# A head's block inverse in one visit to TensorE: four steps for four successive heads at once, in turn by rows

## The chip, the cores and the metric

The kernel runs on one core of a Trainium2 chip, as one launch. The metric is the device time of that launch in microseconds (us). A core has five engines with a queue of instructions each: PE (TensorE, the matrix products; its weight loads are listed apart as PEld), DVE (VectorE), ACT (ScalarE), POOL (GpSimd) and SP (SyncE, which issues the DMAs here). An engine works through its queue in order and waits on semaphores for results of the others.

## What is computed

The program is a trunk of two layers over 512 positions of width 1024. In each layer a gated delta-rule branch (8 heads of width 128) and a sliding-window attention branch run side by side, are merged, and a feed-forward part follows. The change lies in the delta rule, whose core in the reference is a pair of triangular solves for each head and chunk of positions:

```python
kb = k * beta[..., None]
L = jnp.where(strict, jnp.einsum('bhnid,bhnjd->bhnij', kb, k) * decay, 0.0)
u = lax.linalg.triangular_solve(L, v * beta[..., None], left_side=True,
                                lower=True, unit_diagonal=True)
w = lax.linalg.triangular_solve(L, kb * jnp.exp(g)[..., None], left_side=True,
                                lower=True, unit_diagonal=True)
...
def step(state, inp):
    qd, kd, u_c, w_c, a_c, gl = inp
    v_new = u_c - jnp.einsum('bhcd,bhde->bhce', w_c, state)
    o = (jnp.einsum('bhcd,bhde->bhce', qd, state)
         + jnp.einsum('bhij,bhje->bhie', a_c, v_new))
    state = state * jnp.exp(gl)[..., None, None] + jnp.einsum('bhcd,bhce->bhde', kd, v_new)
    return state, o
```

## The kernel before

**The inverse.** The kernel cuts the 512 positions into four chunks (NC = 4) of 128 and builds, for each head and chunk, the inverse of a unit triangular 128x128 matrix, stored as the tile `Pt` (128 x 512, the four chunks side by side). The 32x32 inverses on the diagonal of all heads are made beforehand by `solve`, and stand in `Pc` and, transposed, in `Tc`. The matrix itself (`uu`) lies in DRAM (`ud`). From these parts `d_prep(h)` puts one head's inverse together in four steps. Each step is a group of small fp32 products on TensorE into a bank of PSUM, followed by VectorE instructions that bring the result to SBUF:

- z1 (L964): eight 32x32 products, off-diagonal block times `Tc`, for the rows 0 to 31 and 64 to 95; copied to `zz` (L967).
- p1 (L971, L975): twelve 32x32 products of `zz` with `Pc`; they give the off-diagonal parts of the 64x64 inverses, written to `Pt` (L980) and, transposed, to `T64` (L977).
- z2 (L985): four 64x64 products of the off-diagonal 64x64 block with `T64`, copied to `z2` (L988).
- p2 (L991): four 64x64 products of `z2` with `Pt`; the result is written to the last quarter of `Pt` (L993).

Each step needs the one before, so between two of them TensorE does other work. I call a run of such products between other TensorE work a visit: a head has four. Which rows of the array a product uses is set by the partitions where its operands lie (0, 32, 64 or 96), and the partitions of its output set the columns. `d_prep` also loads `ur` (the head's matrix), `D` and `kk`, clears `Pt` and `T64` on GpSimd and copies the diagonal blocks in, and ends with four transposes of the keys (`ps_kt`, L1000), which ScalarE scales into `kd`.

**The loop over heads.** For head h the code runs `d_prep(h + 1)`, then `d_chain(h)`, the recurrence over four chunks, then steps of the tails of earlier heads, then `d_dense(h + 1)`, three projections of 24 large products each (`ps_qp`, `ps_vp`, `ps_zp`). `d_chain` begins with `ps_qk` (L1067) and transposes of v (`ps_vt`, L1076), and goes on chunk by chunk: y (L1095, which needs `Pt`), su (L1100) and o (L1107), then ks (L1089) and another product into o (L1090). Between two links of this chain VectorE has to bring a result to SBUF.

**What sets the order.** A scheduler orders each engine's instructions when the kernel is built, by priorities and its own estimate of times; what is written one after the other is interleaved. So the large products of `d_dense(h + 1)` stand between the links of `d_chain(h)` and, before, between the visits of `d_prep(h + 1)`. The helper `Order` fixes the order of an engine's instructions between `begin` and `end`, relative to each other.

**Buffers.** PSUM has a bank `pk` (PK, one buffer), which the four steps and `ps_kt` take in turn; `ps` (PS, three), `ss` (PZ, two; `ps_o` is there) and `pm` (PM, two, for the projections). In SBUF `T[2]` has four buffers (`Pt` and `ur`), `X4` six of twice that size. Weights are loaded by SP (`wr`), split by ScalarE (`wh`) and VectorE (`wl`) and used four chunks later at most.

Of the kernel before, what the change touches and what calls it, by code (L numbers as in the profile page):

```python
# [10 lines left out]
F32 = mybir.dt.float32  # L11
# [4 lines left out]
ALU = mybir.AluOpType  # L16
# [103 lines left out]
def hybrid_trunk(ctx, tc, x, positions, pre_mix_g, dn_conv_w, dn_a_log, dn_dt_bias, dn_norm_g,  # L120
# [70 lines left out]
    def c4(ap):  # L191
        return ap.rearrange("p (c i) -> p c i", c=4)
# [67 lines left out]
    def umat(h):  # L260
        return ud[h * NC:(h + 1) * NC, 0:P * P].rearrange("c (j i) -> j c i", j=P)
# [231 lines left out]
    for l in range(depth):  # L493
# [440 lines left out]

        dn = {}

        def d_prep(h):

            Pt = T[2]("Pt")
            nc.gpsimd.memset(Pt, 0.0)  # L940
            T64 = sm.tile([64, 256], F32, name="T64", bufs=1)
            nc.gpsimd.memset(T64, 0.0)
            Ptv, T6v = c4(Pt), T64.rearrange("p (c n) -> p c n", c=4)
            ah = slice(h * NC, (h + 1) * NC)
            ur = T[2]("ur")
            dma(c4(ur), umat(h))
            urv = c4(ur)
            d, k_ = T[3]("D"), T[3]("kk")
            dma(d, dd[h])
            dma(k_, kkd[h])  # L950
            for b in range(4):
                r = slice(b * 32, (b + 1) * 32)
                nc.gpsimd.tensor_copy(Ptv[r, :, r], Pcv[r, ah, :])
            for b in range(2):
                r = slice(b * 32, (b + 1) * 32)
                nc.gpsimd.tensor_copy(T6v[r, :, r], Tcv[r, ah, :])
            yield
            zz = sm.tile([P, 4, 64], F32, name="zz", tag="zz", bufs=2)
            v4 = lambda a: a.rearrange("p (c n) -> p c n", c=4)
            halves = [(slice(b, b + 32), slice(b + 32, b + 64)) for b in (0, 64)]  # L960
            psq = PK("ps_z1")
            for r0, r1 in halves:
                for c in range(NC):
                    mm(psq[r1, c * 32:c * 32 + 32], lhsT=urv[r0, c, r1],  # L964
                       rhs=Tcv[r0, h * NC + c, :], start=True, stop=True)
            for r0, r1 in halves:
                nc.vector.tensor_copy(zz[r1, :, 0:32], v4(psq[r1, 0:128]))  # L967
            psq = PK("ps_p1")
            for r0, r1 in halves:
                for c in range(NC):  # L970
                    mm(psq[r0, c * 32:c * 32 + 32], lhsT=zz[r1, c, 0:32],  # L971
                       rhs=Pcv[r1, h * NC + c, :], start=True, stop=True)
            r1 = halves[0][1]
            for c in range(NC):
                mm(psq[r1, 128 + c * 32:160 + c * 32], lhsT=Pcv[r1, h * NC + c, :],  # L975
                   rhs=zz[r1, c, 0:32], start=True, stop=True)
            ts(out=T6v[r1, :, 0:32], in0=v4(psq[r1, 128:256]), scalar1=-1.0, scalar2=None,  # L977
               op0=ALU.mult)
            for r0, r1 in halves:
                ts(out=Ptv[r0, :, r1], in0=v4(psq[r0, 0:128]), scalar1=-1.0, scalar2=None,  # L980
                   op0=ALU.mult)
            lo_, hi_ = slice(0, 64), slice(64, 128)
            psq = PK("ps_z2")
            for c in range(NC):
                mm(psq[hi_, c * 64:c * 64 + 64], lhsT=urv[lo_, c, hi_], rhs=T6v[lo_, c, :],  # L985
                   start=True, stop=True)
            z2 = sm.tile([P, 4, 64], F32, name="z2", tag="zz", bufs=2)
            nc.vector.tensor_copy(z2[hi_], v4(psq[hi_, 0:256]))  # L988
            psq = PK("ps_p2")
            for c in range(NC):  # L990
                mm(psq[lo_, c * 64:c * 64 + 64], lhsT=z2[hi_, c, :], rhs=Ptv[hi_, c, hi_],  # L991
                   start=True, stop=True)
            ts(out=Ptv[lo_, :, hi_], in0=v4(psq[lo_, 0:256]), scalar1=-1.0, scalar2=None,  # L993
               op0=ALU.mult)
            kds = sm.tile([P, NC], F32, name="kds")
            tc.keep_in_program_order(tt(out=kds, in0=cj[h], in1=c4(d)[:, :, P - 1], op=ALU.mult))
            ps = PK("ps_kt")
            for c in range(NC):
                sl = slice(c * P, (c + 1) * P)
                tr(ps[:, sl], k_[:, sl], ident)  # L1000
# [4 lines left out]
            dn["p", h] = Pt, d, k_, kd  # L1005

        def d_dense(h, after=lambda: None):
            egb = T[6]("egb")
# [50 lines left out]
                    next(tails[h], None)  # L1059

        def d_chain(h):
            Pt, d, k_, kd = dn.pop(("p", h))
            qq, qe, wq, vv, sz = dn.pop(("d", h))
            ps = PS("ps_qk")
            for c in range(NC):
# [300 lines left out]
```

## Time and profile before

| | |
|---|---|
| median of 3 runs | 1878.03 us (1876.44 to 1878.68) |
| profiled execution, own time | 1874.57 us |
| its span, first to last instruction | 1872.9 us |
| mean granted TensorE clock | 0.999 |
| head loop, layer 0 and layer 1 | about 303 to 480 us, 1230 to 1410 us |
| instructions on DVE, ACT, POOL | 2466, 1913, 385 |

A line of the profile names the source line (L964), the engine, the operation, the tiles as output<-inputs (buffer numbers and often digits at the end of a name left out, so that `ps_z` stands for ps_z1 and ps_z2, `ps_p` for ps_p1 and ps_p2, `z` for z2, `T` for T64), the shape and a count. A tile name alone does not tell steps apart; the line does.

### The profile page before, as it was taken

What the parts mean: (1) busy time and instruction counts of PE and PEld (TensorE: products, weight loads), DVE (VectorE), ACT (ScalarE), POOL (GpSimd) and SP (SyncE); (2) the same over time, 40 slices, a digit from 0 to 9 for tenths busy, and PEclk for the clock granted to TensorE, in tenths of its full rate; (3) what the DMA queues carried; (4) which work ended last, traced back from release to release, by engine and by line L of the source; (5) the groups of instructions that cost most, each with busy time, mean ns of one, the idle gap of its engine ahead of it and who ended that gap; (6) DMA issues with size and microseconds to landing.
All of it is one profiled execution on the core that took longest, in us unless ns stands there. A gap on an engine that the chain in (4) does not pass through costs nothing. (4 is left out here: it accounts for less than half of the span.)

```text
span 1872.9 us, 26807 instructions
## 1 busy us (share of the span) xinstructions
PE 1847.6 (99%) x9716; PEld 1534.1 (82%) x9716; DVE 1281.5 (68%) x2466; ACT 939.7 (50%) x1913; POOL 208.1 (11%) x385
## 2 busy tenths in 40 slices
PE   8999999999999999999999999999999999999998
PEld 7888788888888888888888887888888888888886
DVE  5499795777656667684556997857775667586834
ACT  6678732344434645454356887233333346454442
POOL 1322102121100000000012221022111000000000
PEclk9999999999999999999999999999999999999999
DMA  5633436333363253544245333553433533534631
GB/s 179 202 115 117 120 125 196 102 119 109 86 215 127 91 188 97 176 168 170 83 143 188 103 126 105 160 173 102 125 97 110 194 124 99 183 114 158 205 119 45
DMA packets 123445, 255.40 MB, mean 136 GB/s; under 512 B 32609, under 2 KB 49313, under 8 KB 123314
## 3 DMA queue, kind: packets, MB, share of 16 engines
q1 hardware_dynamic: 123314, 253.71, 42.0%
q8 instruction: 76, 1.25, 0.3%
q14 instruction: 55, 0.45, 0.1%
HBM read 224.70 MB, written 28.97 MB: 135 GB/s over the span
## 5 line engine op out<-in xcount | busy, mean ns | idle before, releaser
L320 DVE TENSOR_TENSOR wl<-wr,wh 128x1024 fp32r<-128x1024 f32 (+1 forms) x332 | 402.6, 1222 | 331.2 <-ACT wh L319 323.4
L319 ACT CAST wh<-wr 128x1024 fp32r<-128x1024 f32 (+1 forms) x332 | 344.1, 1041 | 561.8 <-PE ps_f L336 145.9
L335 PE MATMUL ps_f<-g_h,wh 128*128 128x512 f32 x448 | 174.3, 389 | 0.0
L336 PE MATMUL ps_f<-g_l,wh 128*128 128x512 f32 x448 | 174.3, 389 | 0.0
L337 PE MATMUL ps_f<-g_h,wl 128*128 128x512 f32 x448 | 174.3, 389 | 0.0
L397 PE MATMUL ps_p<-wl,P_h 128*128 128x512 f32 x336 | 131.2, 391 | 0.8 <-DVE wl L320 0.8
L399 PE MATMUL ps_p<-wh,P_l 128*128 128x512 f32 x336 | 130.8, 389 | 0.0
L395 PE MATMUL ps_p<-wh,P_h 128*128 128x512 f32 x336 | 129.5, 389 | 0.0
L434 POOL TENSOR_TENSOR pr<-pq,pw 128x1 f32<-128x1 f32 x16 | 9.3, 583 | 809.5 <-DVE pq L433 809.5
L336 PEld LDWEIGHTS ps_f<-g_l,wh 128*128 128x128 f32 x448 | 84.1, 188 | 17.5
L335 PEld LDWEIGHTS ps_f<-g_h,wh 128*128 128x128 f32 x448 | 84.1, 188 | 17.4
L337 PEld LDWEIGHTS ps_f<-g_h,wl 128*128 128x128 f32 x448 | 84.1, 188 | 17.4
L397 PEld LDWEIGHTS ps_p<-wl,P_h 128*128 128x128 f32 x336 | 63.1, 188 | 15.6 <-DVE wl L320 2.3
L395 PEld LDWEIGHTS ps_p<-wh,P_h 128*128 128x128 f32 x336 | 63.1, 188 | 13.3 <-ACT wh L319 0.2
L399 PEld LDWEIGHTS ps_p<-wh,P_l 128*128 128x128 f32 x336 | 63.1, 188 | 12.8
L382 PE MATMUL ps_b<-wh,h_h 128*128 128x432 f32 (+1 forms) x192 | 71.1, 371 | 0.0
L383 PE MATMUL ps_b<-wl,h_h 128*128 128x432 f32 (+1 forms) x192 | 70.4, 367 | 0.0
L384 PE MATMUL ps_b<-wh,h_l 128*128 128x432 f32 (+1 forms) x192 | 70.0, 366 | 0.0
L285 DVE TENSOR_TENSOR wr<-wr 128x1024 f32<-128x1024 f32 x48 | 58.0, 1221 | 2.4 <-DMA wr<-in_weights_dram 1.9
L335 PE MATMUL ps_qp<-h_h,wh 128*128 128x512 f32 x128 | 54.9, 429 | 0.0
L336 PE MATMUL ps_qp<-h_l,wh 128*128 128x512 f32 x128 | 54.1, 423 | 0.0
L864 ACT ACTIVATE M<-M,nm 128x128 f32<-128x128 f32 x128 | 49.8, 391 | 5.9 <-DVE nm L859 5.9
(356 smaller groups left out, 4855.4 us busy)
## 6 DMA issues: line engine op xcount, KB each, us to landing
wr<-in_weights_dram SPq DMA_DIRECT2D x308, 512.0 KB
wr<-in_weights_dram SPq DMA_DIRECT2D x24, 432.0 KB
D<-dd SPq DMA_DIRECT2D x32, 256.0 KB
xd<-xo SPq DMA_DIRECT2D x12, 512.0 KB
xt<-xd SPq DMA_DIRECT2D x24, 256.0 KB
D<-gd SPq DMA_DIRECT2D x16, 256.0 KB
dd<-D SPq DMA_DIRECT2D x16, 256.0 KB
kkd<-kk SPq DMA_DIRECT2D x16, 256.0 KB
```

The costliest lines, as they stand in the source:

```text
L285: tt(out=a, in0=a, in1=o, op=ALU.add)
L319: nc.scalar.copy(wh[:, :w], wr[:, :w])
L320: sub(out=wl[:, :w], in0=wr[:, :w], in1=wh[:, :w].bitcast(F32), op=ALU.subtract)
L335: mm(ps, lhsT=wh[:, k, :], rhs=hi, start=k == 0, stop=False)
L336: mm(ps, lhsT=wh[:, k, :], rhs=lo, start=False, stop=False)
L337: mm(ps, lhsT=wl[:, k, :], rhs=hi, start=False, stop=k == KT - 1)
L382: mm(pss[t], lhsT=hi[:, tsl], rhs=wh[:, r, :], start=k == 0, stop=False)
L383: mm(pss[t], lhsT=hi[:, tsl], rhs=wl[:, r, :], start=False, stop=False)
L384: mm(pss[t], lhsT=lo[:, tsl], rhs=wh[:, r, :], start=False, stop=k == KT - 1)
L395: mm(pss[t], lhsT=hi[:, c], rhs=wh[:, r, :], start=first, stop=False, skip_group_check=onto)
L397: mm(pss[t], lhsT=hi[:, c], rhs=wl[:, r, :], start=False, stop=False, skip_group_check=onto)
L399: mm(pss[t], lhsT=lo[:, c], rhs=wh[:, r, :], start=False, stop=last, skip_group_check=onto)
```

## The change

`d_prep` is split into `d_load` (the loads of a head's matrix), `d_inverse` (the four steps) and `d_keys` (loads of `D` and `kk`, and `ps_kt`). One call `d_inverse(h)` makes, in one bank `ps_i` and one more (`pst`, for the product that is needed transposed), z1 of head h + 3, p1 of head h + 2, z2 of head h + 1 and p2 of head h. The products of z2 and p2 come first, one of each in turn; then those of z1 and p1, in turn by rows. `Order` keeps them in this order. A head's steps so lie in four successive calls, and the calls go from h = -3 to 7; those at the ends hold only the steps whose head exists. `T64` is one tile for the whole program, cleared once. The matrices of up to four heads are held in two `X4` tiles.

```diff
@@ constants
+    T64 = const.tile([64, 256], F32, name="T64")
+    nc.gpsimd.memset(T64, 0.0)
+    T6v = T64.rearrange("p (c n) -> p c n", c=4)
@@ in place of d_prep(h)
+        urs = [X4("ur") for i in range(2)]
+        uview = lambda h: c4(urs[h // 2 % 2][:, h % 2 * 512:(h % 2 + 1) * 512])
+        lo_, hi_ = slice(0, 64), slice(64, 128)
+        r0, r1, r2, r3 = (slice(b * 32, (b + 1) * 32) for b in range(4))
+        v4 = lambda a: a.rearrange("p (c n) -> p c n", c=4)
+        def d_load(*hs):
+            for h in hs:
+                if h < H:
+                    dma(uview(h), umat(h))
+        def d_inverse(h):
+            has = lambda g: 0 <= g < H
+            blk = lambda t_, g, r, c: t_[r, g * NC + c, :]
+            psq, pst = PK("ps_i"), PZ("ps_i")
+            u1, u2 = (uview(g) if has(g) else None for g in (h + 3, h + 1))
+            z1, z2, Pt = dn.get(("z1", h + 2)), dn.get(("z2", h)), dn.get(("p", h))
+            def wide(k):
+                return slice(256 + k * 32, 288 + k * 32)
+            order = Order(nc.tensor)
+            order.begin()
+            for c in range(NC):
+                cw_ = slice(c * 64, (c + 1) * 64)
+                if has(h + 1):
+                    mm(psq[hi_, cw_], lhsT=u2[lo_, c, hi_], rhs=T6v[:, c, :], start=True, stop=True)
+                if has(h):
+                    mm(psq[lo_, cw_], lhsT=z2[hi_, c, :], rhs=c4(Pt)[hi_, c, hi_], start=True, stop=True)
+            for c in range(NC):
+                if has(h + 3):
+                    mm(psq[r1, wide(c)], lhsT=u1[r0, c, r1], rhs=blk(Tcv, h + 3, r0, c), start=True,
+                       stop=True)
+                if has(h + 2):
+                    mm(psq[r0, wide(c)], lhsT=z1[r1, c, 0:32], rhs=blk(Pcv, h + 2, r1, c), start=True,
+                       stop=True)
+                if has(h + 3):
+                    mm(psq[r3, wide(c)], lhsT=u1[r2, c, r3], rhs=blk(Tcv, h + 3, r2, c), start=True,
+                       stop=True)
+                if has(h + 2):
+                    mm(pst[r1, c * 32:c * 32 + 32], lhsT=blk(Pcv, h + 2, r1, c), rhs=z1[r1, c, 0:32],
+                       start=True, stop=True)
+                    mm(psq[r2, wide(c)], lhsT=z1[r3, c, 0:32], rhs=blk(Pcv, h + 2, r3, c), start=True,
+                       stop=True)
+            order.end()
+            if has(h):
+                ts(out=c4(Pt)[lo_, :, hi_], in0=v4(psq[lo_, 0:256]), scalar1=-1.0, scalar2=None,
+                   op0=ALU.mult)
...
+            if has(h + 2):
+                ah = slice((h + 2) * NC, (h + 3) * NC)
+                Pt = T[2]("Pt")
+                dn["p", h + 2] = Pt
+                nc.gpsimd.memset(Pt, 0.0)
...
+        def d_keys(h):
...
@@ the loop
-        fin(d_prep(0))
+        d_load(0, 1, 2, 3)
+        for h in (-3, -2, -1):
+            d_inverse(h)
+        d_keys(0)
         for h in range(H):
+            d_inverse(h)
+            d_load(h + 4)
             if h < H - 1:
-                fin(d_prep(h + 1))
+                d_keys(h + 1)
             d_chain(h)
```

The lines after the change stand three further down in the shared code (L335 becomes L338); in `d_inverse`, L969 is z2, L971 p2, L974 and L980 z1, and L977, L983 and L985 p1; L1025 is `ps_kt`, L1093 `ps_qk`, L1102 `ps_vt`, L1121 y.

TensorE's order before, in layer 0, from the end of the projections for head 1: the inverse of head 2 is put together while head 1's chain starts.

```order
L337 MATMUL ps_zp<-h_h,wl 128x512
L964 MATMUL ps_z_3748<-Tc,ur 32x32 x8
L1067 MATMUL ps_qk<-qq,kk 128x128 x4
L971 MATMUL ps_p_3759<-Pc,zz 32x32 x8
L975 MATMUL ps_p_3759<-zz,Pc 32x32 x4
L1076 MATMUL ps_vt<-ident,vv 128x128 x4
L335 MATMUL ps_qp<-h_h,wh 128x512
L336 MATMUL ps_qp<-h_l,wh 128x512
L337 MATMUL ps_qp<-h_h,wl 128x512
L1095 MATMUL ps_y<-vs,Pt 128x128
L985 MATMUL ps_z_3775<-T_3733,ur 64x64 x4
```

The four runs of small products are apart; the fourth (L991) follows four large products later. After the change the visit h = 2 stands at the end of the projections for head 2. Its 64x64 products end and its 32x32 products begin like this (`z_3803` is z2 of head 2, `z_3805` z1 of head 4):

```order
L969 MATMUL ps_i<-T_96,ur 64x64
L971 MATMUL ps_i<-Pt,z_3803 64x64
L974 MATMUL ps_i<-Tc,ur 32x32
L977 MATMUL ps_i<-Pc,z_3805 32x32
L980 MATMUL ps_i<-Tc,ur 32x32
L983 MATMUL ps_i<-z_3805,Pc 32x32
L985 MATMUL ps_i<-Pc,z_3805 32x32
L974 MATMUL ps_i<-Tc,ur 32x32
```

Before the first row stand six more of the two lines in turn, and behind the last the rest of four rounds of five; nothing lies between. TensorE then goes on with head 2's chain and the transposes of head 3's keys:

```order
L985 MATMUL ps_i<-Pc,z_3805 32x32
L1093 MATMUL ps_qk<-qq,kk 128x128 x4
L1102 MATMUL ps_vt<-ident,vv 128x128 x4
L338 MATMUL ps_qp<-h_h,wh 128x512
L339 MATMUL ps_qp<-h_l,wh 128x512
L340 MATMUL ps_qp<-h_h,wl 128x512
L338 MATMUL ps_qp<-h_h,wh 128x512
L339 MATMUL ps_qp<-h_l,wh 128x512
L340 MATMUL ps_qp<-h_h,wl 128x512
L1025 MATMUL ps_kt<-ident,kk 128x128 x4
L1121 MATMUL ps_y<-vs,Pt 128x128
```

The small products have left the space between qk and y, and `ps_kt`, which takes the same bank as `ps_i`, follows six large products after vt. On VectorE the instructions that empty the bank now follow one another, here for the visit h = 2, between sz (from the projection `ps_zp`) and the first use of `ps_qk`:

```order
L410 TENSOR_TENSOR w_l<-w,w_h 128x512
L1047 SCALAR_TENSOR_TENSOR sz<-sz,ps_zp 128x512
L989 TENSOR_SCALAR Pt<-ps_i 64x4x64
L993 COPY z_4071<-ps_i 64x256
L998 COPY z_4073<-ps_i 32x128 x2
L1009 TENSOR_SCALAR T_96<-ps_i 32x4x32
L1012 TENSOR_SCALAR Pt<-ps_i 32x4x32 x2
L1021 TENSOR_TENSOR kds<-cj,D 128x4
L1097 SCALAR_TENSOR_TENSOR aT<-ps_qk,cj,D 128x128 x4
```

Before, instructions of these sizes stood in four places of VectorE's order, with those for `ps_qk` and y between them.

More of the change, by code (lines that the diff above doesn't have):

```diff
@@ new lines, in hybrid_trunk @@
+        lo_, hi_ = slice(0, 64), slice(64, 128)
[40 more added lines that the diff above has]
+                   op0=ALU.mult)
+            if has(h + 1):
+                z2 = sm.tile([P, 4, 64], F32, name="z2", bufs=1)
+                nc.vector.tensor_copy(z2[hi_], v4(psq[hi_, 0:256]))
+                dn["z2", h + 1] = z2
+            if has(h + 3):
+                z1 = sm.tile([P, 4, 32], F32, name="z1", bufs=1)
+                for r in (r1, r3):
+                    nc.vector.tensor_copy(z1[r], v4(psq[r, 256:384]))
+                dn["z1", h + 3] = z1
+            if has(h + 2):
[3 more added lines that the diff above has]
+                nc.gpsimd.memset(Pt, 0.0)
+                for r in (r0, r1, r2, r3):
+                    nc.gpsimd.tensor_copy(c4(Pt)[r, :, r], Pcv[r, ah, :])
+                for r in (r0, r1):
+                    nc.gpsimd.tensor_copy(T6v[r, :, r], Tcv[r, ah, :])
+                ts(out=T6v[r1, :, 0:32], in0=v4(pst[r1, 0:128]), scalar1=-1.0, scalar2=None,
+                   op0=ALU.mult)
+                for ra, rb in ((r0, r1), (r2, r3)):
+                    ts(out=c4(Pt)[ra, :, rb], in0=v4(psq[ra, 256:384]), scalar1=-1.0, scalar2=None,
+                       op0=ALU.mult)
@@ L950, in d_prep @@
             dma(k_, kkd[h])
[L951 to L992, printed above, removed]
@@ L1061, in d_chain @@
         def d_chain(h):
-            Pt, d, k_, kd = dn.pop(("p", h))
+            Pt = dn.pop(("p", h))
+            d, k_, kd = dn.pop(("k", h))
             qq, qe, wq, vv, sz = dn.pop(("d", h))
```

14 lines of the change are left out of this document (1 added, 13 removed).

## The prediction

> **What bounds the kernel now.** I read the page's line of engines first, then the view of windows over the two stages in which the edited code runs (the loop over the eight heads, once per layer).
>
> ```profile
> span 1872.9 us, 26807 instructions
> PE 1847.6 (99%) x9716; PEld 1534.1 (82%) x9716; DVE 1281.5 (68%) x2466; ACT 939.7 (50%) x1913; POOL 208.1 (11%) x385
> ```
>
> The windows give length, then busy time of PE, PEld, DVE, ACT and POOL, then granted clock and DMA.
>
> ```profile
> 303.00:480.00 177.00, 177.00 (x1287) 143.70 (x1285) 126.06 (x262) 67.91 (x136) 32.89 (x63) 1.00 0.35 109
> 1230.00:1410.00 180.00, 180.00 (x1299) 146.14 (x1299) 127.05 (x264) 69.33 (x138) 31.65 (x62) 1.00 0.36 110
> ```
>
> TensorE is busy for 177 of 177 us and 180 of 180 us, at full clock; VectorE, the next, for 126 of 177. So in these stages the start of each TensorE instruction sets the start of the next, and what counts is not how long a product lasts but how far apart the starts stand. That is read from the timeline of TensorE alone: start, length from first start to last end, line, shape, count. An fp32 product shows as two instructions (passes), so eight of them are x16. Head 0, with its four visits:
>
> ```profile
> 303.30 0.39 PE L337 MATMUL ps_ga<-h_h,wl 128*128 128x512 f32 x1
> 303.62 0.59 PE L964 MATMUL ps_z<-Tc,ur 32*32 32x32 f32 x16
> 304.14 1.16 PE L1067 MATMUL ps_qk<-qq,kk 128*128 128x128 f32 x8
> 305.23 0.49 PE L971 MATMUL ps_p<-Pc,zz 32*32 32x32 f32 x13
> 305.53 0.21 PE L975 MATMUL ps_p<-zz,Pc 32*32 32x32 f32 x1
> 305.56 0.19 PE L971 MATMUL ps_p<-Pc,zz 32*32 32x32 f32 x1
> 305.59 0.19 PE L975 MATMUL ps_p<-zz,Pc 32*32 32x32 f32 x1
> 305.59 0.19 PE L971 MATMUL ps_p<-Pc,zz 32*32 32x32 f32 x1
> ...
> 305.65 0.32 PE L975 MATMUL ps_p<-zz,Pc 32*32 32x32 f32 x5
> 305.90 0.66 PE L1076 MATMUL ps_vt<-ident,vv 128*128 128x128 f32 x4
> ...
> 307.09 0.39 PE L335 MATMUL ps_qp<-h_h,wh 128*128 128x512 f32 x1
> 307.32 0.40 PE L336 MATMUL ps_qp<-h_l,wh 128*128 128x512 f32 x1
> 307.65 0.68 PE L985 MATMUL ps_z<-T,ur 64*64 64x64 f32 x8
> 308.25 0.50 PE L337 MATMUL ps_qp<-h_h,wl 128*128 128x512 f32 x1
> 308.59 0.40 PE L335 MATMUL ps_qp<-h_h,wh 128*128 128x512 f32 x1
> ...
> 310.79 0.60 PE L1000 MATMUL ps_kt<-ident,kk 128*128 128x128 f32 x4
> ```
>
> Undisturbed, a large product starts 0.23 after the one before (307.09 to 307.32). Around a visit there are two losses: entering (307.32 to 307.65 is 0.33, so 0.10) and leaving (308.25 to 308.59 is 0.34, so 0.11), and inside the visit the last start stands well before the next user's.
>
> **What the four visits cost now.** For the lengths of single instructions, and to see that z2 and p2 are alike, the view by source line (ns min/median/max):
>
> ```profile
> L1067 PE MATMUL ps_qk<-qq,kk x128: 270/275/377, 304.1 to 1417.3; 128*128 128x128 f32 x128
> L964 PE MATMUL ps_z<-Tc,ur x256: 191/191/212, 303.6 to 1391.1; 32*32 32x32 f32 x128
> L985 PE MATMUL ps_z<-T,ur x128: 218/218/267, 307.6 to 1395.0; 64*64 64x64 f32 x128
> L991 PE MATMUL ps_p<-Pt,z x128: 218/218/267, 309.4 to 1396.7; 64*64 64x64 f32 x128
> ```
>
> And the pace of the 128x128 products, from a narrower window:
>
> ```profile
> 304.69 0.61 PE L1067 MATMUL ps_qk<-qq,kk 128*128 128x128 f32 x4
> ```
>
> Four qk passes last 0.61, one alone 0.275, so they stand 0.112 apart, and eight undisturbed would take 0.90 to the next start and be 1.06 long.
> - z1: enter 0.32 - 0.23 = 0.09; run 303.62 to 304.14 = 0.52; leave 0.10 (the qk row is 1.16 long, not 1.06). 0.71.
> - p1: enter 0.09 (qk holds 1.09, less 0.90, less the 0.10 just counted); run 305.23 to 305.90 = 0.67; leave 0.06 (vt row 0.66 against 0.60 of the kt row, four transposes each). 0.82.
> - z2: 0.10 + 0.60 + 0.11 = 0.81. p2: the same instruction lengths and form, 0.81.
>
> That is 3.15 us a head, 16 heads: **50.4 us**.
>
> **What the new visits cost.** Inside a run, starts follow the rows of the array. The z2 row is 0.68 long with a last pass of 0.22: eight passes on one row group start within 0.46, and 0.14 passes until the next user. At 305.65 five 32-row passes on one row group are 0.32 long, the last 0.19: 0.032 apart. But where two row groups alternate (305.59 twice, one L971 and one L975) two starts fall within 0.03: each group keeps its own pace, beside the other.
> - 64-row part of a full visit: the z2 and p2 products lie on the two halves of the rows, in turn. I take them side by side: 0.46 for sixteen passes, where before they took two runs.
> - Change from 64-row to 32-row products: no row of before shows one. Below it is bounded by nothing, above by leaving plus entering a large product (0.20). I take 0.14, the time from the last 64-row pass to the next user after z2.
> - 32-row part: rows 32 to 63 carry sixteen passes (the new L977 and L983), every other group eight. Sixteen at 0.032 give 0.50; the others fit beside them. Then 0.12 to the next user (305.65 + 0.32 - 0.19 = 305.78, next start 305.90). If the densest pace shown, two per 0.03, were the limit for all forty passes, it would be 0.64.
>
> A full visit runs 0.46 + 0.14 + 0.50 + 0.12 = 1.22. Per layer there are eleven visits, by the bounds in the code: h = -3 has only eight z1 products on two groups (0.24 + 0.12 = 0.36); h = -2 the 32-row part alone (0.62); h = -1 to 5 both parts (7 x 1.22 = 8.54; an unpaired half costs as much as a pair); h = 6 and 7 only 64-row products (2 x 0.60). That is 10.72, and eleven times entering and leaving (0.195) 2.15: 12.87 a layer, **25.7 us** in all. The products take 24.7 us less.
>
> The Trainium skill, page "TensorE: Matmul & The Clock Gate", section "The mechanism", says that matmuls start in strict program order. The row at 305.53 disagrees: an L975 starts there while L971 passes that stand ahead of it in the program start at 305.56 and later. By the page's rule each 32-row product would hold its neighbour up, twenty products at two passes 0.64 in place of 0.50, and the sum would be 2.2 us higher.
>
> **What becomes late.** Two waits are added to the sum.
>
> First, the chain of a head (y, su, o, ks) is hidden behind large products. Where only two stand between ks and y, y waits:
>
> ```profile
> 369.55 0.39 PE L1107 MATMUL ps_o<-aT,yy 128*128 128x128 f32 x2
> ...
> 370.62 0.47 PE L335 MATMUL ps_qp<-h_h,wh 128*128 128x512 f32 x1
> 370.94 0.40 PE L336 MATMUL ps_qp<-h_l,wh 128*128 128x512 f32 x1
> 371.17 0.48 PE L1095 MATMUL ps_y<-rr,Pt 128*128 128x128 f32 x2
> ```
>
> The y pair is 0.48 long, an unhindered pair 0.39: 0.09. Counting TensorE's order, such places go from 9 to 13 a layer, since p1, z2 and p2 no longer lie in the chain: 8 more waits, about 0.9 us with the smaller ones at ks.
>
> Second, a wait that the trace of before does not have. ps_kt uses the one pk bank, which the visit's ps_i holds until VectorE has emptied it; in the new order kt comes six large products after vt (h = 2 to 4), eleven (h = 1), none (h = 6). Behind kt on TensorE stands everything. Its price needs ScalarE's and VectorE's rows at the same place of a later head:
>
> ```profile
> 384.66 0.59 PE L964 MATMUL ps_z<-Tc,ur 32*32 32x32 f32 x16
> 385.10 0.59 ACT L1021 ACTIVATE sz<-ps_zp 128x512 f32<-128x512 f32 x1
> 385.42 0.59 DVE L967 COPY zz<-ps_z 32x128 f32<-32x128 f32 x2
> 386.05 0.69 DVE L1022 SCALAR_TENSOR_TENSOR sz<-sz,ps_zp 128x512 f32<-128x512 f32 x1
> 387.43 0.58 DVE L980 TENSOR_SCALAR Pt<-ps_p 32x128 f32<-32x128 f32 x2
> 389.18 0.43 DVE L988 COPY z<-ps_z 64x256 f32<-64x256 f32 x1 [0.53 <-PE ps_z L985]
> L993 DVE TENSOR_SCALAR Pt<-ps_p x16: 416/417/417, 310.1 to 1397.0; 64x256 f32<-64x256 f32 x16
> ```
>
> The tanh for sz ends 1.03 after the visit's start, so VectorE takes sz (0.69) at about 1.1, then in its new order Pt 0.42, z2 0.43, z1 0.59, T64 0.29, Pt 0.58: 4.1, with some 0.03 between instructions 4.3. TensorE comes to kt at 1.22 + 0.10 + 0.90 (qk) + 0.36 (vt, three at 0.11 and the step to a large product) + 6 x 0.23 + 0.09 (leaving) = 4.05. So a wait of 0.25 at h = 2, 3 and 4, none at h = 0 and 1, 0.1 at h = 5 (no z1 there, four large products), and at h = 6 VectorE ends at 2.75 while kt comes two transposes after qk, at 1.82: 0.9. That is 1.75 a layer, 3.5 us; bounds nothing (VectorE starts earlier) and 6.5 (0.3 more at each of h = 2 to 6).
>
> Edits at no price: the fourteen clears of T64 that go are GpSimd's, busy 33 of 177 us; the u loads move ahead in SP's queue and to another pool, with up to three heads more in flight, and the first visit stands behind two ga units as before; VectorE's instructions keep their number and sizes. All of it lies behind a TensorE that is never idle; it would cost what TensorE then waits.
>
> Sum, against the profiled execution's 1874.57 (span 1872.9): -50.4 + 25.7 + 0.9 + 3.5 = -20.3, so 1854.3. The median shown is 1878.03, 3.5 higher; with the same saving it becomes **1857.7**.
>
> **Rivals.**
> - A, the 64-row halves do not run side by side: 0.46 more in each paired visit (h = 0 to 6), 14 x 0.46 = 6.4, so 1864.1. For it: before runs z2 and p2 apart, and no row shows two 64-row groups together. Against: the 32-row groups at 305.59 do it.
> - B, "in turn by rows" does not do what it says because products of different rows into one PSUM bank take turns. All four row groups write ps_i. Then a full visit's 32-row part is 32 passes at 0.032 (pst is another bank) or 1.02, 0.52 more in eight visits, 0.24 at h = -3, and rival A on top: 8.8 + 6.4 = 15.2, so 1872.9. Against it: L971 and L975 write the same bank at 305.59. The Trainium skill, page "TensorEngine Tiling (Array Packing)", section "Gotcha 1: PSUM Pressure", says that different row tiles cannot access one bank at the same time; this trace shows that they can, at least for starts.
> - C, slower: the pk wait. If ScalarE reaches the tanh for sz two weight casts later than above, VectorE starts 2.2 later, and each of the 14 visits that kt follows costs TensorE 2.2 us and more: +30.8 against -23.8 (the sum without the 3.5), so 1885. It turns from gain to loss at 1.7 us a visit. For it: one bank, a burst of six evacuations in a row. Against: in ScalarE's new order sz stands right behind w_h for most heads, as now.
>
> **How the numbers follow.** Forecast 0.74 (its own range 1852 to 1863: no kt wait and a free row change give 1852.2, the pace of 0.64 and the dearer kt 1862.9). A 0.10, B 0.06, C 0.04; 0.03 for kt waits near 1.7 that cancel the gain, 0.03 for a mixture of A and the waits that is still faster. Two in ten may be left out: B, C and the last two are 0.16. So 1851 to 1865, with A inside and about 1 us for the scatter of medians (1876.44 to 1878.68). A measurement tells 0.2% (3.8 us) from no change: faster 0.74 + 0.10 + 0.06 + 0.03 = 0.93, same 0.03, slower 0.04.
>
> **What would show it.** Right: sixteen 64-row and forty 32-row passes in one run of about 1.2 us, starts of the new L969 and L971 (p2 there) interleaved, and 0.2 around them; TensorE still without idle time but for kt rows that start late. Wrong: 64-row starts that stay 0.06 apart whichever half they use (A), a 32-row part near 1.0 (B), kt waits of more than a microsecond behind VectorE (C). If the head stages shorten by about 12 us each and the time does not, something outside them gave it back.

## The result and the profile after

| | kernel before | changed kernel |
|---|---|---|
| median | 1877.24 us (1876.14 to 1878.68, 4 runs) | 1857.14 us (1855.52 to 1858.96, 4 runs) |
| ratio, with its 95% interval | | 0.9893 (0.9879 to 0.9907) |
| profiled execution, own time | 1874.57 us | 1856.44 us |

The changed kernel is 1.07% faster, about 20 us. A second comparison gave 0.9888 (0.9875 to 0.9902). The first two lines of the changed kernel's page:

```profile
span 1854.7 us, 26704 instructions
PE 1825.0 (98%) x9716; PEld 1514.8 (82%) x9716; DVE 1280.2 (69%) x2466; ACT 941.2 (51%) x1913; POOL 211.4 (11%) x370
```

TensorE has the same 9716 products, is 22.6 us less busy (1847.6 before), and the span is 18.2 us shorter: some of the gain has come back as idle time. To see where, I cut each layer's head stage out of both traces: from the twentieth TensorE instruction ahead of the first visit to the first ps_ud product behind the heads. The view of windows, first of the kernel before, then of the changed kernel (window, length, then busy time of PE, PEld, DVE, ACT, POOL, then clock and DMA):

```profile
299.00:511.59 212.59, 212.53 (x1462) 172.22 (x1461) 148.30 (x299) 83.54 (x165) 37.39 (x66) 1.00 0.35 106
1227.33:1439.92 212.59, 212.52 (x1462) 172.18 (x1461) 148.33 (x299) 83.54 (x165) 36.09 (x65) 1.00 0.35 107
sum 425.18, PE 425.05 PEld 344.39 DVE 296.63 ACT 167.08 POOL 73.48; mean PE 212.53 PEld 172.20 DVE 148.32 ACT 83.54 POOL 36.74
```

```profile
299.93:501.42 201.49, 200.41 (x1461) 162.39 (x1460) 147.80 (x299) 84.27 (x165) 35.13 (x51) 1.00 0.36 113
1218.54:1420.97 202.43, 201.24 (x1461) 162.36 (x1460) 147.35 (x299) 84.22 (x165) 34.69 (x51) 1.00 0.36 112
sum 403.92, PE 401.64 PEld 324.75 DVE 295.15 ACT 168.50 POOL 69.81; mean PE 200.82 PEld 162.37 DVE 147.57 ACT 84.25 POOL 34.91
```

The head stages are 425.18 - 403.92 = 21.3 us shorter. TensorE, which was idle in them for 0.13 us, is now idle for 403.92 - 401.64 = 2.28. The rest of this single execution is 3.1 us longer than in the one before; the section on the prediction comes back to that.

**A visit of the changed kernel.** TensorE's timeline at head 3 (start, length, line, product). L969 is z2 and L971 is p2, both 64 rows; L974 and L980 are z1, L977 and L985 are p1, L983 is T's product, all 32 rows:

```profile
379.74 0.39 PE L340 MATMUL ps_zp<-h_h,wl 128*128 128x512 f32 x1
380.06 0.27 PE L969 MATMUL ps_i<-T,ur 64*64 64x64 f32 x1
380.06 0.27 PE L971 MATMUL ps_i<-Pt,z 64*64 64x64 f32 x1
380.17 0.22 PE L969 MATMUL ps_i<-T,ur 64*64 64x64 f32 x1
380.17 0.22 PE L971 MATMUL ps_i<-Pt,z 64*64 64x64 f32 x1
...
380.52 0.22 PE L971 MATMUL ps_i<-Pt,z 64*64 64x64 f32 x1
380.67 0.21 PE L974 MATMUL ps_i<-Tc,ur 32*32 32x32 f32 x1
380.68 0.21 PE L977 MATMUL ps_i<-Pc,z 32*32 32x32 f32 x1
380.68 0.21 PE L980 MATMUL ps_i<-Tc,ur 32*32 32x32 f32 x1
380.69 0.21 PE L983 MATMUL ps_i<-z,Pc 32*32 32x32 f32 x1
380.70 0.21 PE L985 MATMUL ps_i<-Pc,z 32*32 32x32 f32 x1
...
380.88 0.19 PE L974 MATMUL ps_i<-Tc,ur 32*32 32x32 f32 x1
380.91 0.18 PE L977 MATMUL ps_i<-Pc,z 32*32 32x32 f32 x1
380.91 0.19 PE L974 MATMUL ps_i<-Tc,ur 32*32 32x32 f32 x1
...
381.03 0.19 PE L985 MATMUL ps_i<-Pc,z 32*32 32x32 f32 x1
381.15 0.71 PE L1093 MATMUL ps_qk<-qq,kk 128*128 128x128 f32 x4
```

What to see: z2 and p2 start together, pass by pass, so their sixteen passes start within 0.46 us. From the last of them to the first 32-row pass it is 0.15. The five 32-row products start within 0.03 of each other, and all forty passes within 0.36 (380.67 to 381.03). The visit ends 1.09 after its start, where qk begins.

**The new wait.** VectorE and TensorE behind the same visit:

```profile
381.00 0.78 DVE L410 TENSOR_TENSOR w_l<-w,w_h 128x512 fp32r<-128x512 f32 x1
381.70 0.67 DVE L1047 SCALAR_TENSOR_TENSOR sz<-sz,ps_zp 128x512 f32<-128x512 f32 x1
382.30 0.41 DVE L989 TENSOR_SCALAR Pt<-ps_i 64x256 f32<-64x256 f32 x1
...
384.07 0.58 DVE L1012 TENSOR_SCALAR Pt<-ps_i 32x128 f32<-32x128 f32 x2
```

```profile
383.75 0.40 PE L340 MATMUL ps_qp<-h_h,wl 128*128 128x512 f32 x1
384.75 0.63 PE L1025 MATMUL ps_kt<-ident,kk 128*128 128x128 f32 x4 [0.61 <-issue]
```

VectorE empties the last part of ps_i until 384.65, and kt, which needs the same bank, starts at 384.75 after 0.61 of idle time. The view names "issue" as what ended it; the bank is inferred from the two rows standing so close. The experiments below ask whether the bank is really the cause.

### The profile page after: what moved, and what is told of

The parts are those of the page before. It is cut to its first block, busy times and chain, and to the rows that moved or that the text cites. A ratio compares the mean times of both kernels' runs of the same rounds, so it can differ in the third digit from the quotient of the medians.

```text
span 1854.7 us, 26704 instructions
## 1 busy us (share of the span) xinstructions
PE 1825.0 (98%) x9716; PEld 1514.8 (82%) x9716; DVE 1280.2 (69%) x2466; ACT 941.2 (51%) x1913; POOL 211.4 (11%) x370
## 4 chain that ended last, share of the span: by engine, by line
PE 83%; DVE 7%; ACT 5%; DMA 2%; issue 2%; POOL 1%; SPq 0%; DVEq 0%; POOLq 0%; ACTq 0%
PE ps_f L338 5%; PE ps_f L339 5%; PE ps_f L340 5%; PE ps_p L400 3%; PE ps_p L402 3%; PE ps_p L398 3%; PE ps_b L385 3%; PE ps_b L387 3%; PE ps_b L386 3%; PE ps_us L338 2%; PE ps_us L339 2%; PE ps_us L340 2%; PE ps_vp L340 2%; PE ps_vp L339 2%; DVE wl L323 2%
## 5 line engine op out<-in xcount | busy, mean ns | idle before, releaser
L338 PE MATMUL ps_f<-g_h,wh 128*128 128x512 f32 x448 | 174.3, 389 | 0.0
L338 PEld LDWEIGHTS ps_f<-g_h,wh 128*128 128x128 f32 x448 | 84.1, 188 | 17.4
L338 PE MATMUL ps_qp<-h_h,wh 128*128 128x512 f32 x128 | 55.0, 429 | 0.0
```

What stands on the lines that cost most here:

```text
L338: mm(ps, lhsT=wh[:, k, :], rhs=hi, start=k == 0, stop=False)
```

## The experiments

The head stages repeat far better than whole executions: the changed kernel run once more, unedited, gave this.

> The changed kernel again, unedited, beside the three others on one chip and to see what of its profile repeats. Theory: a ratio to before of 0.989 again; the head stages (from shortly ahead of the first visit to the first ps_ud product) as long as in its first profile, 201.5 and 202.4 us, within 0.5, so that they can be compared between single profiles; the stages outside them scatter by 1 us. Rival (kt's waits depend on when transfers land): the head stages scatter as the rest does, by 1 us or more.

Measured: ratio 0.9888, head stages 201.48 and 202.20 (201.49 and 202.43 the first time), idle 2.33 (2.28). So they repeat within 0.25 us and are the measure used here, beside the timed ratio. "Small products" is worked out from the single starts in each trace: from a visit's first start to its next user, plus what the intervals on both sides have above the undisturbed pace (0.232 after a 128x512 product, 0.112 after a 128x128 one). Idle is length minus PE busy.

| kernel | median us | ratio to before (95%) | head stages us | idle in them | small products |
|---|---|---|---|---|---|
| before | | 1 | 425.18 | 0.13 | 49.9 |
| changed, first | 1857.14 | 0.9893 (0.9879 to 0.9907) | 403.92 | 2.28 | 23.4 |
| changed, again | 1854.86 | 0.9888 (0.9875 to 0.9902) | 403.68 | 2.33 | 23.3 |
| turn alone, four visits | 1869.29 | 0.9966 (0.9955 to 0.9978) | 418.19 | 0.22 | 43.1 |
| one visit, no turn | 1862.38 | 0.9931 (0.9918 to 0.9943) | 410.57 | 0.00 | 35.1 |
| two visits a head | 1859.48 | 0.9920 (0.9906 to 0.9933) | 406.84 | 3.40 | 25.5 |
| T's product on p1's tile | 1857.19 | 0.9901 (0.9886 to 0.9916) | 404.48 | 0.95 | 25.8 |
| kt in another bank | 1854.87 | 0.9895 (0.9881 to 0.9908) | 403.70 | 2.60 | |
| evacuations on ScalarE | 1855.79 | 0.9894 (0.9880 to 0.9907) | 404.85 | 2.72 | |
| both of these | 1862.49 | 0.9927 (0.9914 to 0.9939) | 411.27 | 9.27 | |
| four z1 copies | 1855.15 | 0.9891 (0.9877 to 0.9905) | 403.07 | 1.97 | |
| evacuations late, kt in another bank | 1853.80 | 0.9884 (0.9871 to 0.9898) | 402.53 | 0.90 | |
| one z1 copy | 1852.22 | 0.9878 (0.9864 to 0.9891) | 400.17 | 0.27 | 23.3 |

Medians of different rows come from different chips, where the kernel before took 1874.9 to 1877.2; ratios are what compares.

### What is "in turn by rows" worth?

**The turn alone**, in the four visits of the kernel before:

```diff
-            for r0, r1 in halves:
-                for c in range(NC):
+            for c in range(NC):
+                for r0, r1 in halves:
                     mm(psq[r0, c * 32:c * 32 + 32], lhsT=zz[r1, c, 0:32], ...)
-            r1 = halves[0][1]
-            for c in range(NC):
+                r1 = halves[0][1]
                 mm(psq[r1, 128 + c * 32:160 + c * 32], ...)
```

(and the same for z1.)

> The kernel before with its four visits a head, and only the products inside z1 and p1 put in turn by rows. TensorE's order is otherwise that of before. Theory (pace by tile): z1 runs 0.37 instead of 0.52, p1 0.40 instead of 0.67, 16 heads: 6.7 us less than the kernel before, 1870.5. Rival (the gain comes from fewer visits alone): 1877, no change.

TensorE's timeline at head 0, z1, qk, p1 and vt:

```profile
305.34 0.44 PE L966 MATMUL ps_z<-Tc,ur 32*32 32x32 f32 x16
305.71 1.16 PE L1072 MATMUL ps_qk<-qq,kk 128*128 128x128 f32 x8
306.79 0.22 PE L976 MATMUL ps_p<-Pc,zz 32*32 32x32 f32 x2
...
307.05 0.19 PE L979 MATMUL ps_p<-zz,Pc 32*32 32x32 f32 x1
307.17 0.66 PE L1081 MATMUL ps_vt<-ident,vv 128*128 128x128 f32 x4
```

z1 runs 0.37 (0.52 before) and p1 0.38 (0.67). Small products fall by 6.8 us, the head stages by 7.0, and the timed ratio is 0.9966, 6.4 us. The theory holds, the rival (only the number of visits counts) falls.

**The visits without the turn**, each step of the changed kernel in one piece:

```diff
-            for c in range(NC):
-                cw_ = slice(c * 64, (c + 1) * 64)
-                if has(h + 1):
-                    mm(psq[hi_, cw_], ...)
-                if has(h):
-                    mm(psq[lo_, cw_], ...)
+            if has(h + 1):
+                for c in range(NC):
+                    mm(psq[hi_, cw_[c]], ...)
+            if has(h):
+                for c in range(NC):
+                    mm(psq[lo_, cw_[c]], ...)
```

(and the same for z1 of each row group, p1 of each, T.)

> The changed kernel with the same visits, but each step's products in one piece instead of in turn by rows (all L969, then all p2 products; all z1 of the first rows, then of the second, then p1, then T). Theory (each tile of the array keeps its own pace of 0.058 us a 64-row pass and 0.032 a 32-row pass, and a product can start at most some four passes ahead of the place where the queue is held): the 64-row part grows by 0.23 us in 14 visits, the 32-row part by 0.38 in 16, 0.13 in two more: 9.5 us more, 1866.6. Rival 1 (the order does not matter, the gain is only that there are fewer visits): 1857. Rival 2 (no product passes another, each piece runs alone): 0.46 and 0.92 more, 21.6 us, 1878.7.

```profile
384.03 0.50 PE L969 MATMUL ps_i<-T,ur 64*64 64x64 f32 x5
384.31 0.27 PE L972 MATMUL ps_i<-Pt,z 64*64 64x64 f32 x1
...
384.54 0.45 PE L972 MATMUL ps_i<-Pt,z 64*64 64x64 f32 x5
384.92 0.49 PE L976 MATMUL ps_i<-Tc,ur 32*32 32x32 f32 x13
...
385.89 0.38 PE L1092 MATMUL ps_qk<-qq,kk 128*128 128x128 f32 x1
```

A full visit runs 1.86 us instead of 1.09. The p2 products (L972) start 0.28 behind the first z2 product, when five of its eight passes have started: pieces overlap only at their ends. So TensorE does not start its passes strictly in the order of its queue, but here a pass overtakes only three that stand ahead of it. This run takes the turn out of the 64-row halves too, which the kernel before did not have. Small products grow by 11.7 us (9.5 expected, so the overlap is a little smaller than supposed), but the head stages by 6.8 and the time by 0.0038 to 0.0043, 7 to 8 us: TensorE's idle time of 2.3 us is gone, and another 2.6 that was spent in lengthened intervals. The intervals ahead of kt, which in the changed kernel are 3.6 us above the undisturbed pace in all, are back at it. Whatever slows TensorE here is partly paid out of the waits.

### What sets the pace of the 32-row part?

The prediction took rows as the limit: sixteen passes on rows 32 to 63, 0.50 us. The trace shows 0.36. T's product and p1's share these rows, but write different columns of the array. In this run they share both:

```diff
-                    mm(pst[r1, c * 32:c * 32 + 32], lhsT=blk(Pcv, h + 2, r1, c), ...)
+                    mm(pst[r0, c * 32:c * 32 + 32], lhsT=blk(Pcv, h + 2, r1, c), ...)
```

> The changed kernel with T's product (L983) written to partitions 0 to 31 of its bank instead of 32 to 63, so that it uses the same 32x32 tile of the array (rows 32 to 63, columns 0 to 31) as the p1 product L977, and not only the same rows; VectorE copies it across. Nothing else changes but the order the scheduler gives kt. Theory (the pace of 0.032 us holds per tile, row and column group): sixteen passes on one tile, 0.26 us more in each of the 16 visits with p1, so the full visit runs 1.35 instead of 1.09 and the time grows by up to 4.1 us, less what kt's waits (1.7 us) give back: 2.4 to 4.1 more. Rival (the pace holds per row group, and the 0.36 was seen for another reason): nothing changes, 1.09 a visit.

```profile
382.15 0.21 PE L977 MATMUL ps_i<-Pc,z 32*32 32x32 f32 x1
...
382.62 0.22 PE L983 MATMUL ps_i<-z,Pc 32*32 32x32 f32 x2
382.77 0.49 PE L1093 MATMUL ps_qk<-qq,kk 128*128 128x128 f32 x2
```

Sixteen passes on one tile now start from 382.15 to 382.65 (the second of the last two stands 0.03 behind 382.62): 0.50, and the visit runs 1.23. At h = 5, where z1 is missing, the visit goes from 0.99 to 1.23, by 0.24, eight passes at 0.03. So the pace belongs to the tile, rows and columns together, and the rival by row groups falls. Columns alone do not set it either: in the changed kernel L974 and L983 write the same columns from different rows, sixteen passes as well, and they too start within the 0.36. My size was wrong: I expected 0.26 more in a full visit and measured 0.14, since without the shared tile the full visit does not keep 0.032 to its end. Its last ten passes stand 0.017 apart on average (380.88 to 381.03 in the rows above), which costs 0.10; at h = 5, with three products in a round, nothing of the kind appears. What makes this tail was not tried. The timed ratio rose by 0.0013, 2.4 us, which is within the intervals; the small products grew by 2.4, and the head stages by only 0.8, since idle time fell by 1.4.

The Trainium skill, page "TensorEngine Tiling (Array Packing)", section "Key Properties", says that different tiles load and multiply in parallel; this run and the visit above agree. The Trainium skill, page "TensorE: Matmul & The Clock Gate", section "The mechanism", says that a weight load overlaps running products only where the row group differs; L977 and L983 have one row group, and the trace shows the weights of L983 being loaded from 380.69 on, while the first L977 pass runs from 380.68 to 380.89, so here the trace decides against it.

### What does one more visit cost?

The 64-row part and the 32-row part as two visits (kt finds its bank free in this order):

```diff
+        def d_inv64(h):
+            psq = PZ("ps_i")
...
+        def d_inv32(h):
+            psq, pst = PK("ps_j"), PZ("ps_j")
...
         for h in range(H):
-            d_inverse(h)
+            d_inv64(h)
             d_load(h + 4)
             if h < H - 1:
                 d_keys(h + 1)
+            d_inv32(h)
             d_chain(h)
```

> The changed kernel with the 64-row part and the 32-row part as two visits (the 64-row part in a bank of the pool of two, so that kt finds the pk bank free). 14 visits more. Theory (a visit's own price is entering, leaving and the way from its last start to the next user, less the 0.15 of the change from 64 to 32 rows that it saves): 0.19 us each, 2.7 us, against 3.7 saved by the free bank: 1856.1, and 2.7 above the kernel with kt in another bank. Rival 1 (a visit costs what z2 and p2 cost before, 0.8): 11 us more, 1864.6. Rival 2 (a visit's price is only its products): like the kernel with kt in another bank, 1853.4.

The two parts run 0.612 and 0.483, 1.095 together, exactly what the one visit runs: the 0.15 at the change from 64 to 32 rows is no more than the way from a last 64-row pass to any other user. What is added is entering and leaving, 2.1 us by the small products (2.7 expected). The time went up by 4.6 us against the kernel with kt in another bank (0.9920 against 0.9895, intervals that just overlap), the head stages by 3.1. Beside the 2.1 stand waits of ks for VectorE's St, 3.4 us in six places, the longest 0.9, where the kernel with kt in another bank has waits of su (next section). A visit's own price is near what was expected; moving it also moved the chain into a worse place.

### What does TensorE wait for behind a visit?

**Another bank for kt.**

```diff
-            ps = PK("ps_kt")
+            ps = PZ("ps_kt")
```

> The changed kernel with one name altered: the transposes ps_kt take a bank of the pool of two (ss) instead of the one pk bank that the visit's ps_i holds; the scheduler then puts kt right behind the visit. Theory (kt waits for VectorE to empty ps_i): the waits of kt in the profile of after, 2.0 us in the first layer and 1.7 in the second, go, so 3.7 us less than the changed kernel: about 1853.4. Rival (the head is late anyway, the same time is then waited at y or ks): within 1 us of the changed kernel, 1856 to 1858, with the y and ks waits grown by as much as kt's shrank.

What TensorE waits for, by the view of waits (total, times, longest), first in the changed kernel, then in this one:

```profile
PE ps_kt L1025 <- issue: 1.7, 6, 0.6
```

```profile
PE ps_su L1126 <- DVE yy L1123: 1.6, 6, 0.6
```

VectorE and TensorE at head 4 of this kernel:

```profile
409.89 0.58 DVE L1012 TENSOR_SCALAR Pt<-ps_i 32x128 f32<-32x128 f32 x2
410.50 0.17 DVE L1021 TENSOR_TENSOR kds<-cj,D 128x4 f32<-128x4 f32 x1
410.70 1.13 DVE L1097 SCALAR_TENSOR_TENSOR aT<-ps_qk,cj,D 128x128 f32<-128x128 f32 x4
411.75 0.28 DVE L1123 COPY yy<-ps_y 128x128 f32<-128x128 f32 x1
```

```profile
412.08 0.49 PE L1126 MATMUL ps_su<-yy,kd 128*128 128x128 f32 x2 [0.60 <-DVE yy L1123]
```

The waits of kt are gone: it now runs right behind the visit, while ps_i is still full, so the bank did cause them. But nothing is gained: 0.9895 against 0.9888, head stages 403.70 against 403.68. My theory of a gain fell and the rival held. Idle time does not show all of it, because a late start also lengthens an interval in which TensorE still counts as busy: the intervals ahead of kt were 3.6 us above the undisturbed pace in all and are now at it, those ahead of su were 0.3 above it and are now 4.0. The yy copy stands on VectorE behind the same evacuations (and behind the four aT), so su waits where kt waited.

**Four of the six evacuations of ps_i on ScalarE** (a seventh, T64's, empties the other bank), to shorten that burst:

```diff
-                    nc.vector.tensor_copy(z1[r], v4(psq[r, 256:384]))
+                    nc.scalar.copy(z1[r], v4(psq[r, 256:384]))
...
-                    ts(out=c4(Pt)[ra, :, rb], in0=v4(psq[ra, 256:384]), scalar1=-1.0, ...)
+                    act(out=c4(Pt)[ra, :, rb], in_=v4(psq[ra, 256:384]), func=AF.Copy, scale=-1.0)
```

> The changed kernel with four of the six instructions that empty a visit's banks (the two z1 copies and the two 32-row parts of Pt) on ScalarE instead of VectorE. Theory (VectorE's burst behind a visit, sz, Pt, z2, z1, T64, Pt, 3.7 us long, is what kt, su and ks wait for, whichever bank kt takes): the burst gets 1.2 us shorter, kt's waits go and y and ks wait less, 2 to 4 us less than the changed kernel. Rival (ScalarE is as close behind, since kd and vs of the same head stand behind the moved instructions): no change, within 1 us, with waits for ScalarE's vs or kd in place of those for VectorE.

> Both edits, the evacuations on ScalarE and kt in a bank of the pool of two. Theory (one cause, VectorE's burst): like the kernel with the evacuations on ScalarE alone, within 1 us. Rival (two causes that hide each other, the bank and the burst): 1.5 to 2 us below it.

With kt in its old bank: no change in time (0.9894; head stages 404.85, about 1 us longer), and kt now waits for ScalarE's Pt. With both edits: 0.9927, 7 us worse than the changed kernel. ScalarE and TensorE of the second:

```profile
386.15 0.55 ACT L1012 ACTIVATE Pt<-ps_i 32x128 f32<-32x128 f32 x2
386.71 1.15 ACT L1028 ACTIVATE kd<-ps_kt,kds 128x128 f32<-128x128 f32 x4
387.73 1.16 ACT L1105 ACTIVATE vs<-ps_vt,irk 128x128 f32<-128x128 f32 x4
```

```profile
388.16 0.49 PE L1120 MATMUL ps_y<-vs,Pt 128*128 128x128 f32 x2 [1.06 <-ACT vs L1105]
```

The moved Pt, then kd, then vs stand in a row on ScalarE, and y waits for vs at five heads of each layer, 0.46 to 1.06 each. Both theories for this pair were wrong, and so was the rival for both edits; the rival for the first (no change) held, though with a wait for Pt and not for vs or kd. ScalarE, busy for only 84 of 201 us, is as close behind in this place as VectorE. The Trainium skill, page "TensorEngine Tiling (Array Packing)", section "PSUM Bottleneck", advises to empty PSUM with both engines once tiling has made TensorE faster; here that gained nothing in one order and lost in the other.

**One copy for z1, or four.** Where a visit has both z1 and p1, their products write all 128 partitions of the bank, so one copy does for two (0.292 instead of 2 x 0.290 us, by the median of these rows in the view by source line); or each is cut in two (four of 0.218):

```diff
-                for r in (r1, r3):
-                    nc.vector.tensor_copy(z1[r], v4(psq[r, 256:384]))
+                if has(h + 2):
+                    nc.vector.tensor_copy(z1, v4(psq[:, 256:384]))
+                else:
+                    for r in (r1, r3):
+                        nc.vector.tensor_copy(z1[r], v4(psq[r, 256:384]))
```

> The changed kernel with one copy of 128 partitions for z1 in place of two of 32 (0.29 us less of VectorE behind every visit with z1 and p1, 12 in all); the scheduler moves kt by some products. Theory (VectorE's time behind a visit is what TensorE then waits for): 0.3 us less at the heads that wait (h = 2 to 4 in each layer), 1 to 2 us less than the changed kernel. Rival (the waits are those of a chain with too few large products between its steps, and only change place): within 1 us of the changed kernel, and the two head stages together at 403 to 405 us.

> The changed kernel with four copies for z1 in place of two (half the columns each), which makes VectorE's burst behind a visit about 0.4 us longer. Theory (VectorE's burst): 0.4 us more at the heads where kt waits already and at some of the others, 2.4 to 4 us more than the changed kernel, less 0.2 at the heads where kt comes one large product later. Rival (the waits only change place): within 1 us.

The head stages with one copy (it applies at 14 visits, not 12), the sum of the two windows:

```profile
sum 400.17, PE 399.90 PEld 324.90 DVE 290.68 ACT 169.53 POOL 69.66; mean PE 199.95 PEld 162.45 DVE 145.34 ACT 84.77 POOL 34.83
```

One copy: idle time 0.27, head stages 3.5 us shorter, twice what I expected. It has the shortest head stages and the lowest ratio of all, 0.9878 (0.9864 to 0.9891) against the changed kernel's 0.9888 and 0.9893; by the timed ratios alone these intervals overlap. Four copies: 0.29 us more of VectorE a visit, and no loss, where I had expected 2.4 to 4: the scheduler, which arranges the products anew for each kernel, put kt one large product later and other large products between other steps of the chain. So the length of the burst does not fix the price. In both runs length and order change together, and how much of the 3.5 us is the one and how much the other stays open.

**The small evacuations behind the head's chain** in the program, kt in the other bank:

```diff
         for h in range(H):
-            d_inverse(h)
+            rest = d_inverse(h)
...
             d_chain(h)
+            rest()
```

> The changed kernel with kt in a bank of the pool of two and the emptying of the 32-row part (z1, T64, 32-row Pt) written behind the head's chain in the program, so that on VectorE the first yy copy no longer stands behind it. Theory (what the chain waits for is VectorE's burst): the waits for yy at su and at ks go, and the head stages get 2 to 4 us shorter than in the changed kernel (403.9). Rival (the chain's own length: the scheduler uses the earlier yy to put fewer large products between the steps, ks and y wait for their own predecessor instead): 403 to 406.

Head stages of 402.53 and an idle time of 0.90: between the two theories, 1.2 us better than the changed kernel, and by the timed ratio (0.9884) not to be told from it. The waits for yy at su are gone; y waits for ScalarE's vs in two places, and the intervals ahead of y are 6.5 us above the undisturbed pace, where they were 3.1 in the changed kernel.

## Why the prediction was right

1857.7 was predicted, 1857.14 measured. The mechanism is the predicted one: the sum of a gain in the small products and a smaller loss in waits. That the totals agree to 0.6 us is partly luck, since the four executions lie 3.4 us apart (1855.52 to 1858.96) and the misses below cancel.

**The small products**: 50.4 to 25.7 predicted, 49.9 to 23.4 measured, so 26.5 us less rather than 24.7. Entering and leaving, the 64-row part (0.46) and the change of rows (0.15 for 0.14) came out as taken. The mis-sized term is the 32-row part, "sixteen at 0.032 give 0.50": it is 0.36, because rows 32 to 63 hold two tiles that run side by side. The rows of before that I used for it could not tell this, since there the row groups and the tiles of neighbouring products changed together.

**The waits**: 0.9 for the chain and 3.5 for kt predicted, together 4.4; 26.5 - 21.3 = 5.2 measured, of which 2.15 is new idle time (2.28 less 0.13) and the rest is hidden in intervals that are longer than the undisturbed pace. By these intervals kt makes 3.6 of it (none before), y, su and ks together 1.1 more than before, and the remaining 0.5 is spread over the large products. So the two terms come out almost as predicted, the one for kt by luck: its mechanism is the predicted one, the sizes by head are not. At h = 2, 3, 4, 5 and 6 the prediction has 0.25, 0.25, 0.25, 0.1 and 0.9; the intervals of the first layer are longer by 0.17, 0.77, 0.40, 0.36 and nothing. At h = 3 of the first layer VectorE begins sz 1.64 after the visit's start, not 1.1, because w_l stands ahead of it, and TensorE idles 0.61 before kt. At h = 6 I expected 0.9, and nothing came: there VectorE takes sz last, and the bank is empty before kt starts.

```profile
454.63 0.42 DVE L989 TENSOR_SCALAR Pt<-ps_i 64x256 f32<-64x256 f32 x1
455.06 0.43 DVE L993 COPY z<-ps_i 64x256 f32<-64x256 f32 x1
455.52 0.69 DVE L1047 SCALAR_TENSOR_TENSOR sz<-sz,ps_zp 128x512 f32<-128x512 f32 x1
```

```profile
455.72 0.60 PE L1025 MATMUL ps_kt<-ident,kk 128*128 128x128 f32 x4
```

What the prediction did not see is that the bank is only the place where the wait shows: taken away, it came back at su.

**Nothing outside the heads** was in the sum. In the first profile these stages took 3.1 us more; in the second execution of the same kernel, 1.7. The stretch ahead of the head stages, whose code the turn-alone kernel leaves as it was, took 296.4 us from the first TensorE instruction in the profile of before and 298.2 in that one. So scatter between executions is large enough for most of this; the kernel before was profiled once, and the cause is not shown. A wait of the first ps_ud products for VectorE's yT, 0.8 us in the first profile of the changed kernel, is not in the second; it was not followed further.

**The rivals.** A (64-row halves one after the other) and B (products of different rows take turns at one PSUM bank) are refuted by the visit above: L969 and L971 start within 0.01, and the five 32-row products, which cover all four row groups and four of which write one bank, within 0.03. A 32-row part of 0.64, which the prediction kept as a bound, did not come either: it took 0.36. C (a pk wait large enough to lose) did not come: the longest wait of kt is 0.61, and 1.7 a visit would have been needed.

Where the 21.3 us come from can be said from two sides. The turn alone, put into the old visits, takes 7.0; the rest, 14.3, is fewer visits and steps that share one. No run splits this rest. An estimate from the single starts: 42 visits fewer at about 0.3 each (0.15 in the kernel with two visits a head, and the 0.15 of the change of rows that it saves) give 12.6; p2 beside z2 saves 0.46 in 14 visits, 6.4; z1 beside p1 saves 0.14 in 14 visits, 2.0 (0.25 and 0.26 from first to last start in the turn-alone kernel, 0.36 together). With the turn's 6.8 that is 27.8, against 26.5 measured in the small products. Taken out of the new visits, the turn costs 6.8 in the head stages but 11.7 in the products, because the faster kernel pays part of it in waits.

## What to carry to other kernels

Count the passes per tile of the array, rows and columns together, and put products that use different tiles next to each other in the program: where they stood in pieces, a pass overtook only the last three ahead of it. When small products become faster on a TensorE that is always busy, list what VectorE and ScalarE must do behind them in order: here the wait that came back belonged to that list and not only to the bank in which it first showed, and moving items to the other engine gained nothing because urgent work stood behind them there. Fewer instructions on the same engine (one copy of 128 partitions for two of 32) went with 3.5 us less in the head stages, but the order changed with them.

## What the runs showed of the hardware that was not expected

- Two 32x32 products on the same rows and different columns start 0.013 us apart (L977 and L983 of the changed kernel); on the same rows and columns their passes stand 0.03 apart (the kernel with T's product on p1's tile).
- Within a round, 32-row products that each go to another tile start 0.005 to 0.007 us apart, and the next pass on one tile stands 0.03 behind its last. With five in a round this holds for some thirty passes, and the last ten stand 0.017 apart on average; with three (h = 5) it holds to the end. The cause is open.
- From the last 64-row pass to the first 32-row pass it is 0.148 us, and to the first pass of a 128x128 or 128x512 product 0.148 as well.
- A VectorE copy from PSUM takes 0.29 us for 32 partitions by 128 elements and for 128 partitions by 128 elements alike, and 0.218 for 32 by 64.
